# A hybrid encoder layer on one core: small TensorE products regrouped, weight splits in quarters, sums in PSUM, a ring of eight tiles

## The chip, the core and the metric

The kernel runs on one core of a Trainium2 chip. A core has TensorE (PE, the matrix products; PEld is its loading of weights), VectorE (DVE), ScalarE (ACT), GpSimd (POOL) and SyncE (SP), which here issues the weight transfers. The metric is the device time of one execution in microseconds (us). The kernel before takes 1457.91 us, the median of 3 runs (1456.87 to 1460.44).

## What is computed

One layer of an encoder trunk for 256 tokens of width 2048, all in float32. The reference, cut to what matters:

```
mod = silu(c) @ w_ada + b_ada                 # six vectors of 2048: shift, scale, gate, twice
h = rms_norm(x, g_mix) * (1 + sc1) + sh1
z = h @ w_in                                  # 2048 x 4616
y = concat[gmlp(u, v), pool(p), forgetting_attention(q, k, va, fz)] @ w_out
x = x + g1 * y
h = rms_norm(x, g_ffn) * (1 + sc2) + sh2
# router: scores = sigmoid(h @ w_router); the best of 4 groups, then its best 2 experts of 4
hid = silu(xb @ w_gate[e]) * (xb @ w_up[e])   # for the tokens of each of 16 experts
x = x + g2 * (scatter of hid @ w_down[e], times the gate)
```

The last 8 columns of `w_in` give `fz`, the forget logits, whose running sum over the tokens enters the attention scores as a bias.

## The kernel before, in words

Numbers are those of the profile's lines. The tokens lie in two halves of 128 (`h`), the width of 2048 in 16 slices of 128 (`k`).

*Weights.* They arrive in tiles of 1 MB, half of a ring tile each (`ring`, L140; six halves until the output projection, then eight), loaded by SP (`load_tile`, L144). There are two kinds. The matrix weights (`w_in`, `w_out`) are split by `split` (L173) into a rounded part on ScalarE (L174) and the rest on VectorE or GpSimd (L175), both in `whl`, and a product is three matmuls (`mm3`, L177). A tile of 512 rows by 512 columns is split in two halves of 128x1024 (`halves`, L407, and `small_piece`, L458); `WSPLIT` and `WSO` say which engine takes the second half's rest. The modulation weights (`w_ada`) go unsplit, either as matmuls with one row of output into an accumulator bank `accs[0]` or `accs[1]`, four slices on the four strips of 32 columns at once (`ada_parts`, L250), or as sums on VectorE in SBUF (`sum_parts`, L272: one operation for each slice, `ga` and `grow`). Which it is stands in `M1A` to `G1`.

*Order.* `step` (L155) issues a load and a split, and puts the work that uses them into a queue `todo`; when more than `LOOK` splits or `LOOK_ALL` loads are queued, the oldest is run. `PLAN` and `LAST` say behind which piece of `w_in` each modulation tile, each chunk's `make_h` and each step of the mixers stands.

*Stages.* The first stage runs over five chunks of slices (`CHUNKS`: 2, 2, 4, 4, 4 slices), since the shift and scale of a chunk are enough to make its part of `h`: the modulation rows of a chunk are copied out (`rows`, L304), turned into columns by four matmuls with one moving column (`cols`, L309), and `make_h` (L386) transposes `x` times the norm by `diag`, applies shift and scale, splits the result and multiplies it by the forget weights into `fzp`, one matmul of 8 rows for each slice (`late`). Then the nine pieces of `w_in` for that chunk are multiplied, each 24 matmuls into two `pm` banks, and added to `z` by `put` (L432). During the last chunk the modulation of the second half (`mod2`) and the mixers run in between: gMLP, pooling with the matrices of `band` (L366), attention in four steps (`att_a` to `att_d`), with the squares of each head summed by `squares` (L539).

The second stage is the output projection: four blocks `n` of 512 columns, four tiles each; behind a block `x1_block` (L836) multiplies by the gate (`xg`) and adds to `x`, then `logit_a` and `logit_b` transpose the new `x` and multiply it by the router weights, with the transposed `x` as the stationary operand. Beside blocks 0 to 2 VectorE sums the gate rows of the following blocks (`grow`), beside block 3 TensorE makes `g2`.

Then come the routing (L945 onwards: scores, group and expert choice, places of the tokens), the gathering of the tokens, and 15 expert places with 24 MB of weights each, whose loads can start only when the routing has written which expert stands where.

## Time and profile before

| | |
|---|---|
| median of 3 runs | 1457.91 us |
| the profiled execution | 1460.89 us |
| its span in the trace | 1459.1 us |
| TensorE busy, granted clock | 1264.6 us, 0.958 |
| VectorE, ScalarE, GpSimd busy | 693.5, 412.8, 146.0 us |
| DMA | 539.14 MB, mean 369 GB/s |

A row of a table by stage gives the length of a stretch, the busy time of PE, PEld, DVE, ACT and POOL with the number of instructions, the granted TensorE clock as a share of 2.4 GHz, the mean busy share of the DMA engines, and GB/s. A row of a timeline gives start, length, engine, line, operation, output and input, and in brackets how long the engine stood idle before it and what released it. A float32 matmul counts as two instructions there, a transpose or a product of split parts as one. Ends of matmuls are modelled and overlap the next start, so that a cost is read from start to start.

### The profile page before, as it was taken

The page shows a single profiled execution, that of the slowest core. Times are in us where ns is not written, and L with a number is a line of the kernel's source. Part 1 is how long each engine was busy: PE and PEld are TensorE (multiplying, and loading weights), DVE is VectorE, ACT ScalarE, POOL GpSimd, SP SyncE. Part 2 cuts the span into 40 slices and gives each one's busy share as a digit, 9 for nine tenths or more (in the row PEclk, how much of TensorE's full clock was granted, in tenths as well). Part 3 has the DMA queues.
Part 4 walks back from the last instruction along what each step waited for, and adds up shares of the span by engine and source line. Part 5 has one row for each costly group of instructions (what it writes and reads, how often), then busy time and mean ns, then how long its engine had stood idle before and what let it go on. Part 6 is the DMA issues. An engine that isn't in the chain of part 4 may idle for free.

```text
span 1459.1 us, 17581 instructions
## 1 busy us (share of the span) xinstructions
PE 1264.6 (87%) x6930; PEld 703.1 (48%) x6930; DVE 693.5 (48%) x1184; ACT 412.8 (28%) x720; POOL 146.0 (10%) x89
## 2 busy tenths in 40 slices
PE   5999999999989997999968999789997879858865
PEld 3666666666667563575324753337633222222221
DVE  3757483555798372795125961169711202202112
ACT  4433333646333240583003840028400000000000
POOL 0423332311333100000000000000000000000000
PEclk8999999999999998999999999999999999979988
DMA  9787787888877868998999989999899999999997
GB/s 378 270 348 281 281 340 265 303 351 328 349 278 270 310 288 367 427 428 317 421 426 427 426 318 419 424 428 426 333 408 428 427 426 427 428 426 428 426 426 303
DMA packets 49207, 539.14 MB, mean 369 GB/s; under 512 B 5464, under 2 KB 5592, under 8 KB 7008
## 3 DMA queue, kind: packets, MB, share of 16 engines
q1 hardware_dynamic: 47664, 534.79, 89.7%
q10 hardware_dynamic: 1456, 3.17, 0.6%
q8 instruction: 56, 0.92, 0.2%
q14 instruction: 31, 0.25, 0.0%
HBM read 535.85 MB, written 2.10 MB: 369 GB/s over the span
## 4 chain that ended last, share of the span: by engine, by line
PE 38%; DMA 27%; DVE 5%; issue 1%; ACT 1%; DVEq 0%; ACTq 0%
PE lbank L170 28%; DMA ring<-in_e_down_dram 11%; DMA ringl<-in_e_gu_dram 9%; DMA ring<-in_e_gu_dram 7%; PE bank L170 5%; PE pm L170 3%; DVE grow L292 2%; PE ada L170 1%; DVE whl L175 1%; DVE el L175 1%; ACT el L174 0%; DVE grow L290 0%; PE lgp L170 0%; DVE hid L1225 0%; PE pt L170 0%
## 5 line engine op out<-in xcount | busy, mean ns | idle before, releaser
L170 PE MATMUL pm<-whl,hT 128*128 128x512 f32 x1120 | 300.9, 405 | 19.9 <-DVE whl L175 10.8
L170 PEld LDWEIGHTS pm<-whl,hT 128*128 128x128 f32 x1120 | 212.3, 193 | 93.6 <-issue 15.3
L170 PE MATMUL lbank<-ringl,xr 128*32 128x256 f32 (+1 forms) x1152 | 143.7, 496 | 38.0 <-DMA ringl<-in_e_gu_dram 37.8
L170 PE MATMUL lbank<-el,xs 128*128 128x512 f32 x576 | 139.9, 401 | 10.2 <-ACT el L174 7.4
L170 PE MATMUL lbank<-ring,xr 128*32 128x256 f32 (+1 forms) x864 | 105.6, 491 | 34.1 <-DMA ring<-in_e_gu_dram 34.0
L174 ACT CAST whl<-ring 128x1024 fp32r<-128x1024 f32 x96 | 99.0, 1048 | 125.7 <-PE pm L170 70.7
L175 POOL TENSOR_TENSOR whl<-ring,whl 128x1024 fp32r<-128x1024 f32 x43 | 108.3, 2518 | 231.7 <-ACT whl L174 211.0
L170 PEld LDWEIGHTS lbank<-el,xs 128*128 128x128 f32 x576 | 109.3, 192 | 41.0 <-ACT el L174 10.6
L170 PE MATMUL bank<-y,gt 128*128 128x512 f32 x240 | 119.1, 619 | 0.0
L1284 DVE TENSOR_TENSOR xa<-xa,bank 128x512 f32<-128x512 f32 x120 | 82.5, 687 | 69.9 <-PE bank L170 69.9
L170 PEld LDWEIGHTS lbank<-ringl,xr 128*32 128x32 f32 (+1 forms) x1152 | 51.9, 128 | 129.8 <-issue 68.5
L170 PE MATMUL lbank<-ring,hidT 128*64 128x512 f32 (+1 forms) x576 | 103.8, 624 | 11.5 <-DMA ring<-in_e_down_dram 11.5
L1275 DVE TENSOR_TENSOR y<-lbank,g2w 128x512 f32<-128x512 f32 x60 | 41.5, 691 | 145.7 <-PE lbank L170 145.7
L174 ACT CAST el<-ring 128x512 fp32r<-128x512 f32 x144 | 89.7, 623 | 29.6 <-PE lbank L170 21.7
L175 DVE TENSOR_TENSOR el<-ring,el 128x512 fp32r<-128x512 f32 x144 | 92.7, 688 | 0.0
L175 DVE TENSOR_TENSOR whl<-ring,whl 128x1024 fp32r<-128x1024 f32 x53 | 72.2, 1368 | 35.9 <-ACT whl L174 33.6
L170 PE MATMUL ada<-ring,cact 128*1 128x512 f32 (+1 forms) x648 | 75.1, 566 | 15.6 <-DMA ring<-in_w_ada_dram 14.4
L1171 ACT COPY gt<-bank 128x256 f32<-128x256 f32 x15 | 5.6, 372 | 287.9 <-PE bank L1169 287.9
L170 PEld LDWEIGHTS lbank<-ring,xr 128*32 128x32 f32 (+1 forms) x864 | 39.5, 128 | 98.4 <-DMA ring<-in_e_gu_dram 48.4
L1225 DVE TENSOR_TENSOR hid<-hid,lbank 128x512 f32<-128x512 f32 x12 | 8.2, 687 | 165.0 <-PE lbank L170 164.7
L170 PE MATMUL lbank<-el,hidT 128*128 128x512 f32 x288 | 74.8, 411 | 12.2 <-DVE el L175 8.3
L438 DVE TENSOR_TENSOR z<-z,pm 128x512 f32<-128x512 f32 x72 | 49.0, 685 | 71.8 <-PE pm L170 71.8
(363 smaller groups left out, 1219.3 us busy)
## 6 DMA issues: line engine op xcount, KB each, us to landing
ringl<-in_e_gu_dram SPq DMA_DIRECT2D x60, 2048.0 KB, 20.1
ring<-in_w_ada_dram SPq DMA_DIRECT2D x90, 1024.0 KB, 7.0
ring<-in_e_gu_dram SPq DMA_DIRECT2D x45, 2048.0 KB, 24.4
ring<-in_e_down_dram SPq DMA_DIRECT2D x45, 2048.0 KB, 25.6
ring<-in_w_in_dram SPq DMA_DIRECT2D x35, 1024.0 KB, 7.0
ringm<-in_e_gu_dram SPq DMA_DIRECT2D x15, 2048.0 KB, 21.7
ringm<-in_e_down_dram SPq DMA_DIRECT2D x15, 2048.0 KB, 21.5
ring<-in_w_out_dram SPq DMA_DIRECT2D x12, 1024.0 KB, 8.3
```

What stands on the lines that cost most here:

```text
L170: E.matmul(out, lhsT=lhsT, rhs=rhs, start=start, stop=stop, skip_group_check=True)
L174: S.copy(hi, src)
L175: (eng or V).tensor_tensor(lo, src, hi.bitcast(F32), op=OP.subtract)
L292: eng.scalar_tensor_tensor(a, w[:, j, :], ck, a, op0=OP.mult, op1=OP.add)
L438: V.tensor_tensor(dst, dst, P[h], op=OP.add)
L1171: S.copy(gt, p[:, :256])
L1225: V.tensor_tensor(hid[:, o], hid[:, o], P[2 * b + 1], op=OP.mult)
L1275: V.tensor_tensor(y, P, g2w[:, c0:c0 + 512], op=OP.mult)
L1284: V.tensor_tensor(a, a, p, op=OP.add)
```

## The change

- `cols4` is new: the columns of a modulation row come by four transposes and a VectorE reduce over the four strips, where they came by four matmuls with a selecting column. `cols` stays for the rows that VectorE sums.
- `make_h` collects the forget matmuls of a chunk, and they run together two entries later in the queue.
- `logit_b` makes the router weights the stationary operand: four matmuls of 16 rows by 256 columns on four strips; at the end the four strips are copied out and added by two matmuls with `sel16`.
- Splits are in quarters (128x512); the look-ahead counts a quarter as 1 and a modulation tile as 2, up to 4; VectorE and GpSimd take the rests in turn.
- `sum_parts` sums into the accumulator banks in PSUM; the last operation writes SBUF.
- Two tiles `spare` join the ring until the last chunk; their room is then `ylo`'s.
- `band` becomes a loop on VectorE ahead of the first chunk; `squares` is one ScalarE operation into a `pt` bank and one reduce on VectorE for each half; `mod2`'s column steps stand two entries later.

```diff
-LOOK, LOOK_ALL = 2, 2
+LOOK, LOOK_SPLITS = 4, 6
-WSPLIT, WSO = "VGGGG", "G"
+WSPLIT, WSO = ["VGVG"] * 5, "VGVG"
...
-        while sum(p for _, _, p in todo) > LOOK or sum(x is not None for _, x, _ in todo) > LOOK_ALL:
+        while sum(0 if x is None else 1 if p else 2 for _, x, p in todo) > LOOK:
             run_first()
...
-    def sum_parts(sec, k0, nk, after, eng, tile_of, bias=None):
+    def sum_parts(sec, k0, nk, after, acc, eng, tile_of, bias=None):
+        P = accs[acc][:, :128 * nk]
...
                     if k == 0:
-                        eng.tensor_scalar(a, w[:, j, :], ck, None, op0=OP.mult)
+                        eng.tensor_scalar(P, w[:, j, :], ck, None, op0=OP.mult)
+                    elif k < KD - 1:
+                        eng.scalar_tensor_tensor(P, w[:, j, :], ck, P, op0=OP.mult, op1=OP.add)
                     else:
-                        eng.scalar_tensor_tensor(a, w[:, j, :], ck, a, op0=OP.mult, op1=OP.add)
+                        a = tile_of()[:, :128 * nk]
+                        eng.scalar_tensor_tensor(a, w[:, j, :], ck, P, op0=OP.mult, op1=OP.add)
...
+    def cols4(r4, nk):
+        p = pt()
+        for m in range(nk):
+            E.transpose(p[:, 128 * m:128 * m + 128], r4[:, 128 * m:128 * m + 128], ident)
+        c = wk.tile([128, 4], F32, name="c4")
+        V.tensor_reduce(c[:, :nk], p.rearrange("p (m j r) -> p m j r", j=4, r=32)[:, :nk, :, 0], AX.X, OP.add)
+        return c
...
+    sp, s_sp = pool("sp", 1, side="right")
+    spare = [sp.tile([128, RINGW], F32, name=f"spare{i}") for i in range(2)]
+    ring_tiles.extend(spare)
...
             split(hq[:, 0, c, :], hq[:, 1, c, :], t)
-            if late is not None:
-                late()
-
-            def late(k=k, t=t):
+            ts.append((k, t))
+
+        def late():
+            for k, t in ts:
                 o = 32 * (k % 4)
                 mm(fzp[o:o + 8, :], wfz[:, k, :], t, start=k < 4, stop=k >= KD - 4)
-        todo.insert(1, (late, None, False)) if todo else late()
+        todo.insert(2, (late, None, False)) if todo else late()
...
-                hl = hp.tile([128, 2, 2, 512], F32R, name="whl")
-                split(hl[:, 0], hl[:, 1], buf[0][:, 2 * a:2 * a + 2, :], engs[a])
+                hl = hp.tile([128, 2, 512], F32R, name="whl")
+                split(hl[:, 0], hl[:, 1], buf[0][:, a, :], engs[a])
...
-            for e in range(4):
-                S.activation(sqj, z[:, h, c0 + 128 * e:c0 + 128 * e + 128], AF.Square,
-                             accum_out=sst[key][:, i, h, e:e + 1])
+            p = pt()
+            S.activation(p, z[:, h, c0:c0 + 512], AF.Square)
+            V.tensor_reduce(sst[key][:, i, h, :], p.rearrange("p (e d) -> p e d", e=4), AX.X, OP.add)
...
-        mod2[i] = (mod2[i][0], 2 + (i // 4 - 1) % 2)
+        mod2[i + 2] = (mod2[i + 2][0], 2 + (i // 4 - 1) % 2)
...
-    mm(lgp.rearrange("p h e -> p (h e)"), maskb[:, :128], ident[:, :32], stop=False)
...
     def logit_b(n):
-        for a in range(2):
-            for c in range(2):
-                for h in range(2):
-                    k = 4 * n + 2 * a + c
-                    mm(lgp[:, h, :], x1T[n][a][:, 256 * c + 128 * h:256 * c + 128 * h + 128], wra[:, k, :],
-                       start=False, stop=k == KD - 1)
+        for j in range(4):
+            k = 4 * n + j
+            mm(lgp[32 * j:32 * j + 16, :], wra[:, k, :], x1T[n][j // 2][:, 256 * (j % 2):256 * (j % 2) + 256],
+               start=n == 0, stop=n == 3)
...
+    lgs = wk2.tile([128, 512], F32, name="x1T", bufs=2)[:, :256]
+    V.tensor_copy(lgs, lgp)
+    lg = pt()
     for h in range(2):
-        V.scalar_tensor_tensor(sc[:, h, :], lgp[:, h, :], rs1[:, h:h + 1], lconst, op0=OP.mult, op1=OP.add)
+        mm(lg[:, 16 * h:16 * h + 16], lgs[:, 128 * h:128 * h + 128], sel16)
+    for h in range(2):
+        V.scalar_tensor_tensor(sc[:, h, :], lg[:, 16 * h:16 * h + 16], rs1[:, h:h + 1], lconst, op0=OP.mult, op1=OP.add)
```

What stands in a row on TensorE where chunk 2 of `h` is made, before (`sel,r`: the columns of the scale; `diag,xa`: a transposed slice; `lgp<-hf`: a forget matmul; a count at the end: so many alike):

```order
L170 MATMUL pt_115<-sel,r_714 128x1 x4
L170 MATMUL pt_114<-diag,xa 128x128 x2
L170 MATMUL pt_115<-diag,xa 128x128 x2
L170 MATMUL lgp<-hf,prm_69 8x256
L170 MATMUL pt_114<-diag,xa 128x128 x2
L170 MATMUL lgp<-hf,prm_69 8x256
L170 MATMUL pt_115<-diag,xa 128x128 x2
L170 MATMUL lgp<-hf,prm_69 8x256
L170 MATMUL pm<-whl,hT_125 128x512 x12
L170 MATMUL lgp<-hf,prm_69 8x256
```

The same place in the changed kernel, on TensorE (`ident,r`: the transposes that replace the columns' matmuls):

```order
L324 MATMUL pt_120<-ident,r_769 128x128 x4
L171 MATMUL pt_119<-diag,xa 128x128 x2
L171 MATMUL pt_120<-diag,xa 128x128 x2
L171 MATMUL pt_119<-diag,xa 128x128 x2
L171 MATMUL pt_120<-diag,xa 128x128 x2
L171 MATMUL pm<-whl,hT_130 128x512 x12
L171 MATMUL lgp<-hf,prm_69 8x256 x4
```

The four forget matmuls have moved together behind two quarters of the first piece.

VectorE in chunk 2 before, where the third and fourth piece meet the shift's last tiles (`whl`: the rest of a split; `z<-z,pm`: the addition of a piece; `ga`: a sum):

```order
L175 TENSOR_TENSOR whl<-ring_64,whl 128x1024
L292 SCALAR_TENSOR_TENSOR ga<-ring_63,cact,ga 128x512 x4
L438 TENSOR_TENSOR z<-z,pm 128x512 x2
L175 TENSOR_TENSOR whl<-ring_63,whl 128x1024
L292 SCALAR_TENSOR_TENSOR ga<-ring_65,cact,ga 128x512 x4
L175 TENSOR_TENSOR whl<-ring_64,whl 128x1024
```

The same place on VectorE in the changed kernel:

```order
L294 SCALAR_TENSOR_TENSOR ada_113<-spare_138,cact,ada_113 128x512 x4
L176 TENSOR_TENSOR whl<-ring_63,whl 128x512
L451 TENSOR_TENSOR z<-z,pm 128x512 x2
L176 TENSOR_TENSOR whl<-ring_65,whl 128x512
L294 SCALAR_TENSOR_TENSOR ada_113<-ring_64,cact,ada_113 128x512 x3
L297 SCALAR_TENSOR_TENSOR ga<-ring_64,cact,ada_113 128x512
```

And on TensorE there, in the changed kernel (`ada_113`: the scale's first matmuls, into the bank that VectorE sums in; `ada_114`: a tile of the second half):

```order
L171 MATMUL ada_114<-ring_63,cact 1x512 x4
L171 MATMUL pm<-whl,hT_130 128x512 x24
L171 MATMUL ada_113<-ring_64,cact 1x512 x4
L171 MATMUL pm<-whl,hT_130 128x512 x24
L171 MATMUL ada_113<-ring_65,cact 1x512 x4
```

The sums have moved from `ga` into `ada_113`, one split now stands on each side of a piece's addition, and TensorE's next matmuls into `ada_113` stand behind the fourth piece, whose addition is the `z` row above.

The end of the projection on TensorE before (`ident,xa`: the transposes of the last block):

```order
L857 MATMUL pt_114<-ident,xa 128x128 x4
L170 MATMUL ada_109<-ring_65,cact 1x512 x4
L170 MATMUL lgp<-wra,x1T 128x16 x8
L170 MATMUL ada_109<-ring_65,cact 1x512 x4
L170 MATMUL ada_109<-ring_63,cact 1x512 x4
```

And in the changed kernel (`sel_91,x1T`: the two matmuls that add the strips):

```order
L873 MATMUL pt_119<-ident,xa 128x128 x4
L171 MATMUL ada_114<-ring_63,cact 1x512 x4
L171 MATMUL lgp<-x1T,wra 16x256 x4
L171 MATMUL pt_120<-sel_91,x1T 128x16 x2
L171 MATMUL ada_114<-ring_63,cact 1x512 x4
```

Two matmuls now stand between the last logits and the modulation tiles behind them.

## Rows read from the trace of the kernel before

**Rows 1.** Table by stage: length, PE, PEld, DVE, ACT, POOL, clock, DMA, GB/s

```profile
20.00:250.00 230.00, 217.72 (x1088) 149.83 (x1084) 139.97 (x188) 78.92 (x100) 72.65 (x44) 0.97 0.78 303
250.00:372.00 122.00, 118.47 (x715) 76.93 (x710) 65.56 (x158) 68.81 (x188) 27.29 (x21) 0.99 0.86 327
372.00:497.00 125.00, 113.88 (x541) 86.51 (x540) 90.41 (x82) 40.86 (x55) 45.34 (x20) 0.95 0.78 302
516.00:1459.00 943.00, 791.27 (x4403) 381.71 (x4402) 379.52 (x674) 211.00 (x357) 0.00 (x0) 0.95 0.96 403
```

**Rows 2.** TensorE's waits, 372 to 497 us: total, times, longest

```profile
PE pm L170 <- DVE xg L839: 7.0, 3, 3.1
PE pm L170 <- DVE whl L175: 3.8, 3, 2.3
```

**Rows 3.** TensorE's waits, 20 to 250 us

```profile
PE pm L170 <- DVE whl L175: 7.0, 6, 2.1
```

**Rows 4.** Timeline of VectorE in the output projection

```profile
417.29 3.10 DVE L292 SCALAR_TENSOR_TENSOR grow<-ring,cact,grow 128x512 f32<-128x512 f32 x4
...
422.04 5.22 DVE L292 SCALAR_TENSOR_TENSOR grow<-ring,cact,grow 128x512 f32<-128x512 f32 x4
```

**Rows 5.** Forms on two tiles: ns shortest/median/longest, first and last start

```profile
L292 DVE SCALAR_TENSOR_TENSOR ga<-ring,cact,ga x30: 739/752/2937, 113.9 to 204.0; 128x512 f32<-128x512 f32 x30
...
L438 DVE TENSOR_TENSOR z<-z,pm x56: 673/686/689, 66.6 to 246.9; 128x512 f32<-128x512 f32 x56
```

**Rows 6.** Timeline of TensorE, and table by stretch as in rows 1

```profile
434.87 0.72 PE L170 MATMUL pm<-whl,hT 128*128 128x512 f32 x1 [2.70 <-DVE xg L839]
...
465.17 0.50 PE L170 MATMUL pm<-whl,hT 128*128 128x512 f32 x1 [3.08 <-DVE xg L839]
...
375.00:380.00 5.00, 5.00 (x12) 3.94 (x13) 3.69 (x5) 0.38 (x1) 0.00 (x0) 0.50 1.01 419
435.00:438.00 3.00, 3.00 (x8) 2.33 (x9) 1.69 (x2) 1.79 (x5) 1.18 (x1) 0.50 0.90 339
465.00:469.00 4.00, 3.83 (x10) 3.08 (x11) 2.12 (x4) 2.49 (x6) 1.28 (x1) 0.59 0.90 358
```

**Rows 7.** Timeline of TensorE: four columns, and four transposes of attention

```profile
87.76 0.95 PE L170 MATMUL pt<-sel,r 128*128 128x1 f32 x8
88.64 1.04 PE L170 MATMUL ada<-ring,cact 128*1 128x512 f32 x8
...
285.30 0.60 PE L567 MATMUL pt<-ident,z 128*128 128x128 f32 x4
285.74 0.39 PE L170 MATMUL pt<-qk 128*128 128x128 f32 x2
```

**Rows 8.** Timeline of TensorE: eight modulation matmuls, a piece, a forget matmul

```profile
41.83 1.04 PE L170 MATMUL ada<-ring,cact 128*1 128x256 f32 x16
42.80 5.74 PE L170 MATMUL pm<-whl,hT 128*128 128x512 f32 x24
...
104.33 0.60 PE L170 MATMUL lgp<-hf,prm 128*8 128x256 f32 x2
104.86 0.71 PE L170 MATMUL pt<-diag,xa 128*128 128x128 f32 x4
```

**Rows 9.** Timeline: a block's logits on TensorE, the first scores on VectorE

```profile
423.40 1.85 PE L170 MATMUL lgp<-wra,x1T 128*128 128x16 f32 x16
425.10 0.48 PE L170 MATMUL pm<-whl,hT 128*128 128x512 f32 x1
...
502.01 0.38 DVE L949 SCALAR_TENSOR_TENSOR sc<-lgp,rs,lconst 128x16 f32<-128x16 f32 x2
```

**Rows 10.** Groups of the page: the experts' splits of 128x512, busy, mean ns

```profile
L174 ACT CAST el<-ring 128x512 fp32r<-128x512 f32 x144 | 89.7, 623 | 29.6 <-PE lbank L170 21.7
L175 DVE TENSOR_TENSOR el<-ring,el 128x512 fp32r<-128x512 f32 x144 | 92.7, 688 | 0.0
```

**Rows 11.** Timeline of TensorE in chunk 2

```profile
126.72 5.26 PE L170 MATMUL pm<-whl,hT 128*128 128x512 f32 x22 [1.51 <-DVE whl L175]
```

More of the change, by code (lines that the diff above doesn't have):

```diff
@@ L209, in body @@
         V.memset(sel[32 * j:32 * j + 1, :], 1.0)
+    sel16 = c1.tile([128, 16], F32, name="sel16")
+    V.tensor_copy(sel16, ident[:, 0:16])
+    for j in range(1, 4):
+        V.tensor_tensor(sel16, sel16, ident[:, 32 * j:32 * j + 16], op=OP.add)
     sel8 = c1.tile([128, 8], F32, name="sel8")
@@ L227, in body @@
     fzp = lgp[:, 256:512]
-    lgp = lgp[:, 0:32].rearrange("p (h e) -> p h e", h=2)
+    lgp = lgp[:, 0:256]
     def pm():
@@ L388, in make_h @@
         hq = hbuf(q)
-        late = None
+        ts = []
         for c in range(nk):
@@ L422, in run @@
                 for h in range(2):
-                    for c in range(2):
-                        xh, xl = xs(2 * a + c, h)
-                        mm3(P[h], xh, xl, hl[:, 0, c, :], hl[:, 1, c, :], first and a + c == 0, last and a + c == 2)
-                if a == 1:
+                    mm3(P[h], *xs(a, h), hl[:, 0], hl[:, 1], first and a == 0, last and a == 3)
+                if a == 3:
                     after(P)
             step(prep, run, True)
-        one(0)
-        one(1)
+        for a in range(4):
+            one(a)
     def put(q, c0, P):
@@ L453, in banks, with one @@
             return P
-        halves(win_d, WIN[q, c0], (V, WS[q]), lambda c, h: hpart(q, c, h), banks, True, True,
+        halves(win_d, WIN[q, c0], WS[q], lambda c, h: hpart(q, c, h), banks, True, True,
                lambda P: put(q, c0, P))
     def small_piece(q, c0, n):
-        buf = []
-        def one(a):
+        buf, P = [], []
+        def one(a, c):
             def prep():
-                if a == 0:
+                if a + c == 0:
                     w = ring()[:, :2 * n]
@@ L466, in prep @@
                     buf.append(w.rearrange("p (k n) -> p k n", k=2))
-                hl = hp.tile([128, 2, 2, 512], F32R, name="whl")
-                split(hl[:, 0], hl[:, 1], buf[0][:, :, 512 * a:512 * a + 512], (V, WS[q])[a])
+                hl = hp.tile([128, 2, 512], F32R, name="whl")
+                split(hl[:, 0], hl[:, 1], buf[0][:, c, 512 * a:512 * a + 512], WS[q][2 * (a % 2) + c])
                 return hl
             def run(hl):
-                P = [pm(), pm()]
+                if c == 0:
+                    P.extend([pm(), pm()])
                 for h in range(2):
-                    for c in range(2):
-                        mm3(P[h], *hpart(q, c, h), hl[:, 0, c, :], hl[:, 1, c, :], c == 0, c == 1)
-                put(q, c0 + 512 * a, P)
+                    mm3(P[2 * a + h], *hpart(q, c, h), hl[:, 0], hl[:, 1], c == 0, c == 1)
+                if c:
+                    put(q, c0 + 512 * a, P[2 * a:])
             step(prep, run, True)
         for a in range(n // 512):
-            one(a)
+            for c in range(2):
+                one(a, c)
     hold = {}
@@ L707, in body @@
                 piece(q, PIECES[i])
-            if q == 0 and i < 4:
-                then(lambda i=i: band(i))
             for c in PLAN[q][i]:
@@ L723, in body @@
     tbanks.append(accs[0])
+    for t in spare:
+        while ring_tiles[-1] is not t:
+            ring_tiles.rotate(-1)
+        ring_tiles.pop()
+    s_sp.close()
+    py, s_py = pool("py", 1, side="right")
+    ylo = py.tile([128, KD, T], F32R, name="ylo")
     work = {
```

61 lines of the change are left out of this document (26 added, 35 removed).

## The prediction

> **What bounds the kernel now.** I read the busy time by stage first [rows 1]. From 516 us to the end the experts run, and there the DMA engines are busy 0.96 of the time at 403 GB/s: weights arrive as fast as they can. The change doesn't touch that stage, and its first load can't start before the routing is known. So whatever is won or lost before 516 us moves the end by the same amount. Before 516 us it is the other way round: from 20 to 497 us the DMA share is 0.78 to 0.86, and TensorE is busy 217.7 of 230, 118.5 of 122 and 113.9 of 125 us. The reader is to see stages where DMA has 14 to 22% to spare, VectorE 28 to 46% and ScalarE 44% or more, and where TensorE works nearly without a hole. Two things can be had there: shorter TensorE work, and the holes.
>
> The holes come next, in the list of waits. In the output projection (372 to 497 us) TensorE stands 7.0 us for `xg`, the DVE multiplication that frees the accumulator banks, and 3.8 us for `whl`, the split weights [rows 2]. From 20 to 250 us it stands 7.0 us for `whl` [rows 3]. All of these are VectorE being late. The timeline of VectorE tells why: four sums of `grow` take 3.10 us at 417.29, but 5.22 us at 422.04 [rows 4]. The form list says the same: a sum takes 752 ns in the median and up to 2937 ns, while `z<-z,pm`, which has one operand in PSUM, stays between 673 and 689 ns in all 56 cases [rows 5], though GpSimd is busy a third of that stretch [rows 1]. So operations with both inputs in SBUF are held up beside GpSimd, and those with one PSUM operand are not.
>
> After the longest of these waits the clock is low as well: after the wait of 2.70 us at 434.87 the granted clock is 0.50 (1.2 GHz) for 3 us, 0.50 for 5 us from 375, 0.59 for 4 us from 465 [rows 6]. Half of such time is lost: 2.5 + 1.5 + 1.6 = 5.6 us.
>
> **The change part by part**, against the profiled execution (1460.9 us; its span is 1459.1).
>
> *Columns by transposes.* Four columns of a modulation row are now four matmuls with one moving column each; from their start to the next instruction 87.76 to 88.64 = 0.88 us [rows 7]. The four 128x128 transposes of attention are the same form as the new ones and take 285.30 to 285.74 = 0.44 us [rows 7]. The order shows twelve sets of four and four sets of two that change (the two sets behind a VectorE sum keep the old form): 12 x 0.44 + 4 x 0.22 = 6.2 us of TensorE. VectorE gets 16 small reduces more; they stand ahead of the `mod` additions, about 0.2 us each, where TensorE has the `diag` products to do.
>
> *Forget logits by chunk.* Sixteen matmuls of 8 rows stand singly between others: 104.33 to 104.86, 0.53 us each, 8.5 us in all [rows 8]. In the new order they follow one another in each chunk, on four different strips of columns. What that gives is shown by the modulation matmuls, one row each, 256 columns, on the same four strips: eight of them take 41.83 to 42.80 = 0.97 us, so a round of four costs 0.5 us [rows 8]. Five chunks, five rounds: 2.5 us, a saving of 6.0.
> The Trainium skill ("TensorE: Matmul & The Clock Gate", "Measured speedup vs the span model") gives 2.38 times for three column tiles, short of three. By an estimate from that, four strips would run 3.2 times as fast as one after another, a round would cost 0.66 us, and the nine rounds here and in the next part would save 1.4 us less; the trace's modulation matmuls do better than the page, 8 x 0.53 / 0.97 = 4.4 times.
>
> *Router weights stationary.* Eight matmuls with 16 moving columns and a 128x128 weight load each take 423.40 to 425.10 = 1.70 us per block of 512 columns [rows 9]. They become four of 256 columns on four strips, by the same row 0.5 us: 3 x 1.2 = 3.6 us saved in the first three blocks, and the 0.2 us matmul that cleared the bank. The fourth stands at the end, where the scores start at 502.01 [rows 9] behind the root of the norm, so its saving there is worth nothing; and behind it come a copy of 256 columns from PSUM (half the width of `z`'s 0.69 [rows 5], so 0.4 to 0.5), two small matmuls at 0.53 at most each [rows 8] and two hand-overs. I take 1.3 us longer for the routing chain. TensorE's remaining modulation work now waits behind those two matmuls, which costs the same time once, not twice. Net 2.5 us.
>
> *Sums in PSUM.* The trace has no VectorE sum into PSUM. Bounds: 0.69 us (`z<-z,pm` [rows 5]) and 1.3 (a quarter of the stretched 5.22 [rows 4]). I take the unstretched 0.75, nearer to `z`, since it too has one SBUF input. Of the projection's waits and lost clock, 7.0 + 3.8 + 5.6 = 16.4 us, most should go: a block of 512 columns has 16 sums (12.0 us), 8 split quarters (5.5) and five more operations of that width (3.5 by the row of `z`): 21 us of VectorE against 96 matmuls, 22.7 us at 5.7 for 24 (the 5.74 at 42.80 [rows 8]), and some 2 us of small ones on TensorE. I leave 1.7 us of the first wait (2.3 today; VectorE does routing constants ahead of it, and the split is now half as long) and 0.2 us at each bank change: 16.4 - 2.3 = 14.1 won. Bounds 8 (the clock not won back) to 16.4.
>
> *The new wait.* The sums now share accumulator `ada_113` with TensorE. In chunk 2 (CHUNKS[2], 110 to 170 us) the order has the last sum right behind a piece and TensorE's next use of that bank right behind the same piece. VectorE must first add that piece to `z` (0.69 [rows 5]), split a quarter (0.69 [rows 10]) and do four sums (3.0): with hand-overs TensorE stands 4.6 us, and every matmul queued behind it with it. At that length it restarts at the low clock, 1.5 us more [rows 6]. In chunk 3 a whole piece (24 matmuls, 5.7 us) lies between and hides the sums. Of the 7.0 us of `whl` waits [rows 3], chunk 2 has two, 1.51 at 126.72 [rows 11] and one like it of 1.93; shorter splits and unstretched sums leave about 1.4 there (VectorE needs 0.7 + 1.4 + 0.7 + 3.0 = 5.8 us for a piece of 5.7, so it stays just late) and 0.8 elsewhere. Sum: 1.4 + 0.8 + 4.6 + 1.5 - 7.0 = 1.3 us lost.
>
> *Splits in quarters.* For half the width there are rows from the experts: ScalarE 623 ns, VectorE 688 ns [rows 10]. A tile then costs ScalarE 2.5 us and VectorE 1.4 us, GpSimd about 2.5, beside 24 matmuls of 5.7 us; nobody becomes the bound. The cover is those 5.7 us; without it the longest of the three, 2.5 us, would show on each tile. The look-ahead keeps its bytes (four quarters for two halves). Nil.
>
> *Ring of 8, bands ahead of time, squares by two operations.* The heads of the two lists of waits stand in [rows 2, 3], and no DMA is in them: TensorE doesn't wait for a tile there, so two more tiles give nothing. The bands (24 short VectorE operations, some 6 us by my estimate) fall where VectorE waits for the first modulation; at worst 1 us is late. The squares take ScalarE work away and give VectorE ten reduces, between 250 and 372 us, where it is busy 65.6 of 122 us [rows 1]. Nil, one microsecond either way.
>
> Sum: 6.2 + 6.0 + 2.5 + 14.1 - 1.3 = 27.5 us. That is 1433.4 us against the profiled execution, which lies 3 us above the median of the runs; against the median 1457.9 it is 1430.
>
> **The rivals.**
> *TensorE's freed time comes back, the holes stay* (VectorE is still late at the banks, through the reduces and the finer splits in its queue): 6.2 + 6.0 + 2.5 - 1.3 = 13.4 us, 1444.5. For it: VectorE is busy 90 of 125 us there and its queue is in order. Against it: `z` is never stretched.
> *The strips don't overlap* for 8- and 16-row weights (the change doesn't do what it says): 6.0 lost, and logits 16 x 0.53 = 8.5 instead of 2.0, of which the last block counts little: 11 us less, 1441.5. Against it: the modulation rows.
> *Slower: sums into PSUM are slow.* One mechanism: each sum reads and writes PSUM, and VectorE becomes the bound in chunks 2 and 3 and in the projection. A block then costs 9.0 + 16x us with x per sum, against 434.87 to 465.17 = 30.3 today [rows 6]; a piece 2.8 + 4x (two splits and two additions of 0.69) against 5.7 and its share of the waits, 0.9; the hand-over 1.6 + 4x. Three blocks, eight pieces and the hand-over give 3 x (9 + 16x - 30.3) + 8 x (2.8 + 4x - 6.6) + 1.6 + 4x = 84x - 92.7 us, and what is won outside them is about 10: it turns at x = 1.22. At twice my price (1.5) the kernel is 23 us slower: 1481. Against it: `z` at 0.69 with a PSUM operand.
> *More than forecast*: no low clock at the new wait, no wait at the projection's start, 1420.
>
> **How the numbers follow.** Forecast 1430 (1423 to 1438 with its own bounds): 0.60. Holes stay, 1444: 0.16. No overlap, 1441: 0.07. Better, 1420: 0.07. Slower, 1481: 0.05. The gains are used up by waits I haven't seen, 1458: 0.05. The range reaches from the good case, 1420, to the holes' case with its own spread, 1448. About 0.3% (4.4 us) is what a measurement of this kernel can tell from no change: faster 0.88, same 0.06, slower 0.06.
>
> **What would show it.** Right: the routing's end at about 489 instead of 516 us with an unchanged stretch behind it; `z`-like durations (0.7 to 0.8 us, hardly a stretched one) for the sums; `xg` waits below 1 us in all; transposes of 0.44 us per four; one TensorE wait of 4 to 5 us on the sum's last step in chunk 2. Wrong: sums over 1.2 us; `lgp` groups of four at 2 us; waits on `pt` banks from the squares; a stretch behind the routing that is not 943 us.

## The result, and the profile after

The changed kernel takes 1439.01 us, the median of 4 runs (1435.49 to 1442.07); the kernel before took 1457.39 us in the 4 runs beside it. The ratio is 0.9874, with a 95% interval of 0.9848 to 0.9899. Faster was forecast, at 1430, with a range of 1420 to 1448: the direction and the range hold, but 18 us came (20.1 in the profiles, up to the first expert load) where 27.5 were forecast.

Three marks cut the trace where the forecast's terms meet: TensorE's first product with `ylo` opens the output projection, the start of its last `pm<-whl` product closes it, and SP's first load of expert weights starts the stretch that the DMA engines bound. Behind that load both kernels take as long, 942.6 us before and 943.8 after [rows 1], so all is decided ahead of it.

| stretch | before | after | forecast | measured |
|---|---|---|---|---|
| to the first product with `ylo` | 372.26 | 358.29 | -10.9 | -14.0 |
| the projection | 123.66 | 112.46 | -17.9 | -11.2 |
| last product to first expert load | 20.54 | 25.64 | +1.3 | +5.1 |
| sum | 516.46 | 496.39 | -27.5 | -20.1 |

VectorE's forms in the changed kernel, as in rows 5: the sums, and the rests of the splits.

```profile
L294 DVE SCALAR_TENSOR_TENSOR ada<-ring,cact,ada x54: 742/756/757, 105.5 to 434.8; 128x512 f32<-128x512 f32 x54
...
L176 DVE TENSOR_TENSOR whl<-ring,whl x86: 677/693/1803, 25.4 to 450.2; 128x512 fp32r<-128x512 f32 x86
```

No sum is stretched any more: the longest takes 757 ns, where one in SBUF took up to 2937 [rows 5]. The splits, with two inputs in SBUF, are still held up, to 1803 ns. The Trainium skill ("SBUF — State Buffer", "Who interferes with whom") says that a VectorE instruction with two SBUF inputs contends with a GpSimd instruction that reads SBUF, and one with at most one does not; these two rows agree.

The new wait in chunk 2, on TensorE and on VectorE:

```profile
120.06 2.56 PE L171 MATMUL pm<-whl,hT 128*128 128x512 f32 x10 [0.65 <-DVE whl L176]
127.04 1.04 PE L171 MATMUL ada<-ring,cact 128*1 128x512 f32 x8 [4.41 <-DVE ga L297]
128.01 7.29 PE L171 MATMUL pm<-whl,hT 128*128 128x512 f32 x24
```

```profile
121.98 1.37 DVE L451 TENSOR_TENSOR z<-z,pm 128x512 f32<-128x512 f32 x2 [1.97 <-PE pm L171]
123.27 0.68 DVE L176 TENSOR_TENSOR whl<-ring,whl 128x512 fp32r<-128x512 f32 x1
123.87 2.33 DVE L294 SCALAR_TENSOR_TENSOR ada<-ring,cact,ada 128x512 f32<-128x512 f32 x3
126.24 0.75 DVE L297 SCALAR_TENSOR_TENSOR ga<-ring,cact,ada 128x512 f32<-128x512 f32 x1
```

It is the forecast's wait, 4.41 us for 4.6: VectorE idles 1.97 us for the piece's end, and then adds, splits and sums while TensorE stands. The 24 products behind it take 7.29 us instead of 5.7.

TensorE's waits in the projection (358 to 471 us), as in rows 2:

```profile
PE pm L171 <- DVE xg L855: 3.7, 3, 1.8
PE pm L171 <- DVE whl L176: 3.0, 1, 3.0
```

7.0 + 3.8 us have become 3.7 + 3.0. Behind the projection 5.1 us were lost where 1.3 were forecast; TensorE there:

```profile
474.98 1.04 PE L171 MATMUL lgp<-x1T,wra 128*16 128x256 f32 x8
477.69 0.62 PE L171 MATMUL pt<-sel,x1T 128*128 128x16 f32 x4 [1.68 <-DVE x1T L963]
478.24 2.38 PE L171 MATMUL ada<-ring,cact 128*1 128x512 f32 x16
480.56 1.86 PE L171 MATMUL ada<-bgt,ident 8*1 8x512 f32 x2
482.35 3.59 PE L171 MATMUL ada<-ring,cact 128*1 128x512 f32 x16
...
488.79 0.62 PE L171 MATMUL pt<-M,ones 128*128 128x16 f32 x4
...
495.26 1.01 PE L171 MATMUL ada<-bgt,ident 8*1 8x512 f32 x2
```

VectorE has `M` ready at 484.79, yet TensorE's products on it start at 488.79, since its `g2` tiles run until then, some at half the clock (1.90 us for 16 entries at the high one). And who releases the first expert load? SP's queue, its start and its waits:

```profile
496.39 0.89 SPq L1312 DMA_DIRECT2D ringl<-in_e_gu_dram  x2
```

```profile
SPq L1316 <- DVE pos L1045: 11.2, 1, 11.2
...
SPq L1312 <- PE ada L171: 3.6, 1, 3.6
```

Its last wait is 3.6 us for TensorE's last modulation product (495.26 + 1.01), not for the routing's `pos`, which is ready at 492.18. It was so before the change too: `pos` at 512.24, the last product's end at 516.34, the load at 516.46. TensorE's queue is the path at the end of the routing.

### The profile page after: what moved, and what is told of

It reads as the page before. It is cut to its first block, busy times and chain, and to the rows that moved or that the text cites. A ratio compares the mean times of both kernels' runs of the same rounds, so it can differ in the third digit from the quotient of the medians.

```text
span 1440.2 us, 17629 instructions
## 1 busy us (share of the span) xinstructions
PE 1247.2 (87%) x6844; PEld 683.4 (47%) x6844; DVE 693.2 (48%) x1271; ACT 417.1 (29%) x754; POOL 160.5 (11%) x127
## 4 chain that ended last, share of the span: by engine, by line
PE 59%; DMA 26%; DVE 7%; issue 3%; ACT 2%; POOL 1%; SPq 0%; DVEq 0%; ACTq 0%; POOLq 0%
PE lbank L171 29%; PE pm L171 18%; DMA ring<-in_e_down_dram 11%; DMA ringl<-in_e_gu_dram 7%; DMA ring<-in_e_gu_dram 7%; PE bank L171 6%; PE ada L171 4%; PE pt L171 1%; DVE ada L294 1%; DMA ring<-in_w_ada_dram 1%; DVE whl L176 1%; DVE el L176 1%; ACT whl L175 1%; DVE z L451 1%; POOL whl L176 0%
## 5 line engine op out<-in xcount | busy, mean ns | idle before, releaser
L171 PE MATMUL pm<-whl,hT 128*128 128x512 f32 x1120 | 296.6, 400 | 9.7 <-DVE whl L176 3.9
L171 PEld LDWEIGHTS pm<-whl,hT 128*128 128x128 f32 x1120 | 208.8, 190 | 82.9 <-issue 12.8
L176 POOL TENSOR_TENSOR whl<-ring,whl 128x512 fp32r<-128x512 f32 x86 | 120.0, 1407 | 225.4 <-ACT whl L175 201.9
L175 ACT CAST whl<-ring 128x512 fp32r<-128x512 f32 x172 | 99.9, 622 | 72.6 <-PE pm L171 62.5
L171 PE MATMUL lbank<-ring,hidT 128*64 128x512 f32 (+1 forms) x576 | 104.6, 630 | 10.9 <-DMA ring<-in_e_down_dram 10.9
L176 DVE TENSOR_TENSOR whl<-ring,whl 128x512 fp32r<-128x512 f32 x86 | 83.9, 991 | 38.0 <-ACT whl L175 37.7
L171 PE MATMUL ada<-ring,cact 128*1 128x512 f32 (+1 forms) x568 | 68.6, 585 | 19.7 <-DMA ring<-in_w_ada_dram 14.0
L175 ACT CAST el<-ringl 128x512 fp32r<-128x512 f32 x96 | 58.7, 624 | 79.5 <-DMA ringl<-in_e_gu_dram 64.8
## 6 DMA issues: line engine op xcount, KB each, us to landing
ringl<-in_e_gu_dram SPq DMA_DIRECT2D x60, 2048.0 KB, 20.1
```

The lines of the kernel that those rows point to most:

```text
L171: E.matmul(out, lhsT=lhsT, rhs=rhs, start=start, stop=stop, skip_group_check=True)
L175: S.copy(hi, src)
L176: (eng or V).tensor_tensor(lo, src, hi.bitcast(F32), op=OP.subtract)
```

## The experiments

Each but one starts from the changed kernel. Single runs of one kernel spread by 2 to 11 us, so stretches of the trace decide on terms of a few microseconds. From the first expert load to the end all profiles show 939.5 to 945.0 us. The expectations name the start of the gathering's second half as the routing's end; it is 500.09, 502.27, 500.46 and 510.14 us in the first four kernels. It proved a poor measure: it contains a low clock that comes and goes (last section), so that the stretch from the last product to the first expert load varies from 22.4 to 27.3 us where nothing was changed in it. The readings below go by the stretches ahead of it.

### One part undone: columns, forget logits, logits, sums

**cols_back**

```diff
-            hold[i] = lambda: fin(cols4(r4, nk))
+            hold[i] = lambda: fin(cols(r4, nk, sel))
```

> The changed kernel with one part undone: the columns of the modulation rows come from four matmuls with one moving column again instead of four transposes and a reduce. Measure: the routing's end, which is the start of the second half's gathering product (499.12 us in the changed kernel, 519.18 before). Theory: a set of four is 0.88 instead of 0.44 us on TensorE and nothing else changes, 12 x 0.44 + 4 x 0.22 = 6.2 us: routing's end 505.3, time about 1445. Rival A: TensorE waits for the reduces (0.95 us for c in the list of waits, and hand-overs), so that the part is worth 3 to 4 us only: 502.5. Rival B: the 3 us by which the stretch before the projection came out better than forecast belong to this part: 508.5.

1441.45 us (ratio 0.9873). The projection opens at 359.91 (+1.6), though the first piece starts 1.0 us earlier: the part is worth 2.6 us, below rival A. Why can be seen where chunk 2 is made, on TensorE with transposes (the changed kernel) and with matmuls (this one), and on VectorE in the changed kernel:

```profile
92.46 0.60 PE L324 MATMUL pt<-ident,r 128*128 128x128 f32 x4
92.90 0.61 PE L171 MATMUL pt<-diag,xa 128*128 128x128 f32 x4
94.10 0.71 PE L171 MATMUL pt<-diag,xa 128*128 128x128 f32 x4 [0.59 <-DVE c L326]
```

```profile
91.53 0.95 PE L171 MATMUL pt<-sel,r 128*128 128x1 f32 x8
92.33 0.69 PE L171 MATMUL pt<-diag,xa 128*128 128x128 f32 x4
```

```profile
92.68 1.27 DVE L451 TENSOR_TENSOR z<-z,pm 128x512 f32<-128x512 f32 x2
93.88 0.16 DVE L326 TENSOR_REDUCE c<-pt 128x4 f32<-128x16 f32 x1
94.08 0.16 DVE L338 TENSOR_TENSOR mod<-c,prm 128x4 f32<-128x4 f32 x1
94.54 0.55 DVE L411 TENSOR_SCALAR hf<-pt,mod 128x256 f32<-128x256 f32 x1
```

Four transposes do take 0.44 us, but at a chunk's turn VectorE's additions and then its chain to `hf` are what is waited for, with the reduce now in it. What TensorE saves there it waits. Of the 2.6 us 1.9 come in the last chunk (132.35 for 134.21 us), where eight of the twelve sets of four stand and the forecast had 3.5: TensorE saves 3.2 on them and waits 0.8 longer in all.

**forget_back**: `make_h` runs each forget matmul behind the next slice again.

```diff
-            ts.append((k, t))
+            if late is not None:
+                late()
...
-            for k, t in ts:
+            def late(k=k, t=t):
```

> The changed kernel with one part undone: each forget matmul stands singly again, behind the next slice of its chunk, instead of all of a chunk together. Theory: 16 x 0.53 us against five rounds of 0.5 to 0.55, 5.7 to 6.0 us: routing's end 505.0 (499.12 in the changed kernel). Rival A: the strips hardly overlap, or the single matmuls fill time in which TensorE waits for the next slice's split: 1 to 2 us, 500.5. Rival B: the single ones also hold up make_h, and the 3 us by which the stretch before the projection came out better than forecast belong here: 508.

1443.22 us (0.989). The projection opens at 364.44, 6.15 us later, of which 1.6 are a low clock (0.69 from 242 to 247 us, 1.00 at that place in the changed kernel). Chunks 0 and 1 are as long as with the part (67.4 us), the others 1.2, 1.4 and, without the clock, 2.0 longer: 4.6 us in all. A round on four strips takes 0.55 us (99.91 to 100.46 in the changed kernel), so the price was right; but of the two-slice chunks nothing comes. By the estimate worked out from the Trainium skill's factor ("TensorE: Matmul & The Clock Gate", "Measured speedup vs the span model") a round would have been 0.66; the measured one is shorter.

**logit_back**

```diff
-            mm(lgp[32 * j:32 * j + 16, :], wra[:, k, :], x1T[n][j // 2][:, 256 * (j % 2):256 * (j % 2) + 256],
+                    mm(lgq[:, h, :], x1T[n][a][:, 256 * c + 128 * h:256 * c + 128 * h + 128], wra[:, k, :],
...
-    V.tensor_copy(lgs, lgp)
```

> The changed kernel with one part undone: in the router logits the transposed x is the stationary operand again, eight matmuls of 16 columns for each half block, with no strips to add at the end. Theory from the trace: the first three blocks lose 3 x 1.15 us (1.70 against 0.55) and 0.2 for the cleared bank, but the end wins back 5.1 us (from the last block's first modulation tile to the routing's end 22.94 us before, 28.05 now): routing's end 497.6, TensorE's wait for the copy of the logits gone, and the matmuls on M within 0.5 us of M's being ready. Rival, the step of the forecast (3.6 + 0.2 won, 1.3 lost): 501.6, with the end still as long as now, since it is long for another reason.

1440.32 us (0.986), no difference that the times could tell. In the trace both halves of the theory are there: the projection is 1.7 us longer (114.19), not 3.65, because `xg` waits shrink from 1.74 to 1.09 us at two bank changes; the stretch behind it is 2.9 us shorter (22.79), and TensorE reaches `M` 0.4 us after it is ready. But 1.6 of the 2.9 us are low clock, of which both profiles have some in this stretch, in different places. Where the clock is high as far as `M`, TensorE goes from the projection's last product to its first product on `M` in 13.50 us here (475.29 to 488.79) and in 14.75 with the part, in scale_later (466.78 to 481.53): 1.25 us, the forecast's 1.3. The part's net worth is 0.5 us by that, and below zero in the changed kernel's profile, where 2.5 were forecast.

**gate_sums_sbuf**

```diff
+        sb = bias is not None
...
+                P = buf[0] if sb else P0
```

> The changed kernel with the 48 sums of the gate rows in SBUF again; the sums of the first stage stay in PSUM. Theory: sums are stretched again beside GpSimd (some to 2.9 us), VectorE comes late to the banks, and the output projection gets back what it won besides the logits: from its first matmul to the modulation tile behind its last block it is 109.4 us now and was 121.3 before, of which 3.4 are the logits, so +8.5: routing's end 507.6. By the size in the forecast (14.1): 513. Rival: the quarters of the splits, taken in turn by VectorE and GpSimd, did it, and the place of the sums matters little: 499 to 501, with sums that are hardly stretched.

1452.59 us (0.995). The projection is 122.85 us, 10.4 longer. The sums' form, and TensorE's waits there:

```profile
L298 DVE SCALAR_TENSOR_TENSOR grow<-ring,cact,grow x33: 739/752/1798, 364.8 to 440.4; 128x512 f32<-128x512 f32 x33
```

```profile
PE pm L171 <- DVE xg L859: 8.2, 3, 3.8
PE pm L171 <- DVE whl L176: 3.0, 1, 3.0
```

With the same quarters and the same queue, the place of the gate rows' sums alone raises the `xg` waits from 3.7 to 8.2 us; most of the other 5.9 us are low clock behind two of them (0.66 from 389 to 394, 0.58 from 448 to 456; 1.00 behind all three in the changed kernel). The rival falls.

### One part alone

**sums_psum_alone** is the kernel before with `sum_parts` of the changed one (the edit is that function's part of the diff).

> The kernel before with one part of the change alone: the modulation sums of VectorE are in the accumulator banks in PSUM; halves of splits, ring, logits, columns and forget products stay as before. Measure: from the first product with ylo to the start of the last product of the projection, 123.7 us before, 112.5 in the changed kernel. Theory: the place of the sums does it nearly all: 113 to 115, sums unstretched at 0.75 us; and in chunk 2 a wait of about 4 us on the sum's last step appears, so that chunk 2 is longer than its 67.2 us of before. Rival: halves of 128x1024, stretched on VectorE, still hold up the banks and the quarters are needed too: 118 or more.

1451.96 us (0.9948). The projection takes 116.07 us, 7.6 less than before and just outside the theory's band. In it lies a stretch of half clock behind no wait, in none of the others' projections:

```profile
479.00:485.80 6.80, 6.80 (x19) 5.50 (x19) 0.00 (x0) 0.37 (x1) 0.00 (x0) 0.50 0.51 212
```

It costs 3.4 us, more than the 1.9 that lie between this projection and that of the changed kernel with the old logits (114.19). So these two profiles don't show that the quarters are worth anything there. Sums are 743 to 757 ns, and the wait appears here too:

```profile
134.59 1.89 PE L170 MATMUL ada<-ring,cact 128*1 128x512 f32 x8 [4.95 <-DVE ga L292]
```

Chunk 2 grows from 67.2 to 73.3 us, so 6.1 us of the sums' gain go there: most of it for this hand-over, some for a low clock (0.70 from 122 to 127 us) behind a `whl` wait ahead of it. `xg` waits are 0.69 us here, one multiplication, against 1.74 with the finer splits: a bank change with its multiplication cost no less than that in these two profiles.

### Parts priced at nothing

**ring_six**

```diff
-    ring_tiles.extend(spare)
```

> The changed kernel without the two extra ring tiles: six ring tiles until the output projection, as before. Measure: the first product with ylo, which opens the output projection (358.3 us in the changed kernel, 372.3 before), and chunks 0 and 1, from the first piece to the first transposed slice of chunk 2 (25.45 to 92.90 = 67.5 us; before 27.06 to 101.65 = 74.6). Theory of the forecast: two more tiles are worth nothing, since TensorE waits for no tile there: 67.5 and 358.3, each within 1 us. Rival: in chunk 0 the DMA engines are busy all the time now (1.01, 0.84 before), so the extra tiles take in weights that chunks 1 and 2 then don't wait for: 70 to 72, and 361 to 363.

1439.49 us (0.9866). Chunks 0 and 1 take 67.43 us: nil, as forecast. The projection opens 2.6 us later, but that arises in chunk 2, at the hand-over (5.07 us, then 0.50 of the clock for 5 us, 0.66 in the changed kernel), and it is as late in logit_back, which has the full ring. In chunk 0 the DMA share falls to 0.83 to 0.89 between 36 and 52 us, from 1.02 with the two extra tiles; nobody waits for what these bring.

**bands_back**: `band` of the kernel before, behind the first four pieces.

```diff
+            if q == 0 and i < 4:
+                then(lambda i=i: band(i))
```

> The changed kernel with the pooling matrices made during chunk 0 again, by VectorE and GpSimd, instead of ahead of it by VectorE. Measure: chunks 0 and 1, 67.5 us in the changed kernel and 74.6 before. Theory: in the kernel before, the last band's four operations (2.7 us) stood on VectorE's queue ahead of the first columns' addition, TensorE waited 0.96 us for it and 1.11 us for a split, and went on at a lower clock: 70 us, with such a wait at the first transposed slice of chunk 1. Rival, the forecast's nil: 67.5, and the 7 us of difference in these two chunks have to do with the quarters and the clock at the start.

1449.35 us (0.9941), 10 us lost. Chunks 0 and 1 take 79.96 us, more than in the kernel before; neither expectation saw it. TensorE, and GpSimd ahead of the first of the waits:

```profile
38.73 1.20 PE L171 MATMUL pm<-whl,hT 128*128 128x512 f32 x4 [2.58 <-POOL whl L176]
48.26 2.07 PE L171 MATMUL pm<-whl,hT 128*128 128x512 f32 x4 [2.59 <-POOL whl L176]
58.56 1.20 PE L171 MATMUL pm<-whl,hT 128*128 128x512 f32 x4 [1.77 <-POOL whl L176]
```

```profile
30.63 0.34 POOL L386 IOTA hf<- 128x256 f32 x1
34.78 0.73 POOL L390 TENSOR_TENSOR band<-hf,tri 128x256 f32<-128x256 f32 x1 [3.80 <-DVE hf L389]
...
37.41 1.26 POOL L176 TENSOR_TENSOR whl<-spare,whl 128x512 fp32r<-128x512 f32 x1
```

GpSimd waits 3.80 us for VectorE's part of a band, with a split queued behind it. In the kernel before, `WSPLIT` gave all rests of chunk 0 to VectorE, so nothing of TensorE's stood behind a band; with "VGVG" two quarters of each tile do. Moving the bands is what the quarters need; what it gives with the old splits was not run.

### What the terms that went wrong are worth

**scale_later**

```diff
-    ["n", "n", "nm", "nn", "n", "n", "n", "0m", "1h"],
+    ["n", "n", "nm", "n", "nn", "n", "n", "0m", "1h"],
```

> The changed kernel, with the scale's first modulation tile of chunk 2 one piece later in the plan, so that 24 matmuls lie between the shift's last sum and TensorE's next use of that accumulator bank. Measure: chunk 2, from the first transposed slice of its h to that of the next chunk: 92.90 to 162.96 = 70.1 us in the changed kernel. Theory of the hand-over: the wait of 4.41 us on the last sum goes, and the low clock behind it (1.5 us in that trace, up to 4 in the ones since) with it: 64 us, and the end moves by 6. Rival: VectorE is the bound over the four pieces with sums (four sums, two splits and two additions are 5.8 us for a piece of 5.7), and TensorE waits for whl where it waited for the sum: 68 us, the end 2 earlier.

1430.24 us (0.9804, interval 0.9783 to 0.9825), 8.8 us below the changed kernel. Chunk 2 takes 64.46 us, 5.6 less; TensorE there now:

```profile
117.07 3.02 PE L171 MATMUL pm<-whl,hT 128*128 128x512 f32 x12 [1.04 <-DVE whl L176]
120.71 8.01 PE L171 MATMUL pm<-whl,hT 128*128 128x512 f32 x34 [0.61 <-DVE whl L176]
```

The rival's waits are there, 1.65 us in all, but not in place of the 4.41. The first expert load comes 7.3 us earlier: 5.6 from here, 3.3 from the end (22.35 us instead of 25.64, where the clock stayed high), less 1.5 us in the last chunk, where it was 0.67 over 5 us behind a wait of 1.35 us. Only the 5.6 are the edit's.

**tail_mend**

```diff
+    def mid(copy):
+        copy()
+        logit_b(3)
+        V.tensor_copy(lgs, lgp)
+
-    logit_a(3, root_x1)
+    logit_a(3, lambda copy: root_x1(lambda: mid(copy)))
     g2_run(G2_MID)
-    logit_b(3)
```

> The changed kernel, with the last block's logits, and the copy of the four strips behind them, placed on VectorE's queue ahead of the four small operations that finish the norm's root (which wait for ScalarE anyway), and the modulation tile that stood before the logits placed behind them. Measure: from the start of the last product of the projection (470.75) to the routing's end (499.12): 28.4 us in the changed kernel, 23.3 before. Theory: the wait of 1.68 us for the copy falls below 0.5, TensorE goes on at the high clock, its matmuls on M start within 0.7 us of M's being ready: 24.0 us. Rival: the low clock at this place comes from the many small matmuls and not from the wait, 27 us.

1440.06 us (0.9879). To the gathering's second half 26.98 us: the theory's 24.0 is missed. Its first part holds: no wait ahead of `sel`, and `M`'s products start 0.7 us after `M`. But then the clock falls, behind a wait of 1.03 us that was there before:

```profile
488.51 0.60 PE L171 MATMUL pt<-ohc,ec 16*128 16x16 f32 x2 [1.03 <-DVE ohc L1039]
489.04 6.52 PE L171 MATMUL ada<-ring,cact 128*1 128x512 f32 x32
495.49 1.01 PE L171 MATMUL ada<-bgt,ident 8*1 8x512 f32 x2
```

6.52 us for 32 entries that take 3.61 at the high clock: what was saved ahead of `M` is lost behind it. The rival's 27 us are met, but not as it had it: ahead of `M` the clock stays high. Why it falls behind `ohc` here, and not in the changed kernel, stays open.

**consts_later**: `wra`, `revc`, `triE`, `capR`, `limR` and GpSimd's index rows in a function called at

```diff
+            if n == 0 and g == 1:
+                consts()
```

> The changed kernel, with the constants of the routing (GpSimd's six index rows, VectorE's wra, revc, triE, capR and limR) issued behind the second tile of the output projection instead of ahead of its first split. Measure: from the first product with ylo (358.29) to block 1's first wait (389.15): 30.9 us in the changed kernel. Theory: VectorE reaches the first rests some 2.6 us earlier, the wait of 2.97 us falls to 0.5, and the half clock of the twelve matmuls behind it, 2.5 us, goes too: 26 us. Rival: the wait is one on the first tile's transfer or on ScalarE's cast, or the constants hold up the splits of the second and third tile as long: 29 to 31.

1439.81 us (0.9874). From the first product with `ylo` to block 1 28.25 us instead of 30.86: between theory and rival. VectorE in the changed kernel, ahead of the wait of 2.97 us:

```profile
358.44 1.41 DVE L826 TENSOR_TENSOR triE<-ioE,ioR 128x256 f32<-128x256 f32 x1
...
359.94 1.07 DVE L834 TENSOR_SCALAR limR<-capR 128x16 f32<-128x16 f32 x1
360.92 2.96 DVE L176 TENSOR_TENSOR whl<-ring,whl 128x512 fp32r<-128x512 f32 x3
```

Without the constants TensorE waits 1.15 us, and the clock behind it is 0.66 for 5 us instead of 0.50. In the times the gain doesn't show, and the projection opens 1.6 us later than in the changed kernel, with a low clock in the last chunk (0.69 over 5 us from 237.6).

**mended** has these three edits.

> The three edits scale_later, tail_mend and consts_later together. Theory: they lie in three different stretches, all before the routing's end, so they add: 6 + 4.4 + 4.9 = 15 us, routing's end at 484 to 486 us instead of 499.1, time 1423 to 1426, ratio to the kernel before 0.977. Rival: the time won early is given back as waits for weights, since transfers start earlier by less: routing's end 491 or later, DMA share above 0.95 from 360 us on.

1428.45 us (0.9805, interval 0.9784 to 0.9825; 5 runs, 1427.93 to 1433.12). The gathering comes at 486.52, 12.6 us earlier, just outside the theory's 484 to 486, and the time misses its 1423 to 1426. The low clock behind `ohc` is there (6.30 us for 3.61), as in tail_mend. The times don't tell it from scale_later alone.

**best** adds two edits for that end:

```diff
-                    mm(P[0:1, :], ident[0:8, bias:bias + 1], bgt, start=False)
+                    mm(P[0:1, :], ident[0:8, bias:bias + 1], bgs[-1], start=False)
...
-    oneh = wide_ring[-1][:, :1024].rearrange("p (h s) -> p h s", h=2)
+    oneh = wide_ring[-1][:, RINGW:RINGW + 1024].rearrange("p (h s) -> p h s", h=2)
```

> The kernel with the three mended places (scale later, logits ahead of the root's end, constants later), and two more edits for the end of the routing: the bias rows that TensorE adds to g2 are read from a copy in memory that the experts' first tile doesn't take over, and the placement matrix stands in the half of its ring tile that the last modulation tile doesn't use. Theory: the first load of expert weights and the placement matrix then no longer wait for TensorE's last modulation products; the load starts within 1 us of VectorE's pos instead of behind the last bias product, 3 us earlier than with the three edits (484.1), at 479 to 481 us, the gathering at about 484, and the time is 1423 to 1426. Rival: the load waits for another reader of that memory or the transfers of the last modulation tiles, and starts at 484 as with the three edits: 1428.

1426.42 us (6 runs, 1423.55 to 1427.31; ratio 0.977, interval 0.9742 to 0.9799), 0.4 us above the theory's band, with every run below all of mended's, and 31 us less than the kernel before. VectorE's `pos`, SP's first load, and TensorE's last bias product:

```profile
480.11 0.19 DVE L1056 COPY pos<-pt 128x48 f32<-128x48 f32 x1
```

```profile
480.92 0.89 SPq L1323 DMA_DIRECT2D ringl<-in_e_gu_dram  x2
```

```profile
486.02 1.01 PE L171 MATMUL ada<-bgs,ident 8*1 8x512 f32 x2
486.96 3.29 PE L171 MATMUL pm<-ring,xa 128*128 128x256 f32 x14
```

The load starts 0.8 us behind `pos` and 6 us ahead of TensorE's end; from the projection's last product it takes 18.09 us, where mended has 24.36 (the projection itself closes 3 us later than there). 943.8 us from it to the end are what the other kernels show. So it was that product, through the memory of `bgt`, that held the load. The second edit came with it and was not run apart; it bears on `ring`, where VectorE waited 2.25 us for TensorE in mended before it wrote the placement matrix and no longer does, while the load goes into `ringl`. The gathering is later than expected (486.96 for 484), since it stands behind the modulation on TensorE's own queue; that costs nothing.

## Why the prediction was right or wrong

*What bounds the kernel*: right. What was won before the first expert load came off the end (20.1 us there, 18.9 in the span), and the stretch behind it didn't change. But that the first load can't start before the routing is known names the earlier of two conditions: it starts behind TensorE's last `g2` product, 4.2 us after `pos`.

*Columns*, 6.2 forecast, 2.6 measured. The step took TensorE's time, from a set's start to the next instruction, for the path. At a chunk's turn VectorE is the path, and the cover that the forecast named for the reduces ("TensorE has the `diag` products to do") ends after one slice, with 0.59 us of wait. In the last chunk about half of it came.

*Forget logits*, 6.0 forecast, 4.6 measured without the clock: price and overlap right, the two-slice chunks give nothing.

*Router logits*, 2.5 forecast, about 0 measured. Two steps failed. In the blocks TensorE's saving was taken for the path: 1.7 came for 3.8, the rest ran into `xg` waits. At the end the 1.3 us were right at the high clock (1.25, by logit_back), but the sum had no term for the clock. The modulation tiles behind the two matmuls are themselves the path to the load, and of the 5.1 us lost in the changed kernel's profile 3.3 are their low clock (25.64 against 22.35 us in the profiles whose clock stays high there). Another 0.6 of the 5.1 are not the logits': TensorE waits 0.78 us for `xa` ahead of the last transposes, where it waited 0.28, and does so with the old logits too. Nor is it shown that the logits cause the low clock: in logit_back, tail_mend, mended and best the wait for the copy is gone, and the clock falls behind `ohc` instead.

*Sums in PSUM and the projection*: mechanism right, price right (0.756 for 0.75), 10.4 us by the undone part and 7.6 alone, with 3.4 us lost to a half clock behind no wait in it. The term of 14.1 was too large at two places. First wait: 1.7 forecast, 2.97 measured and 2.5 us of half clock behind it,

```profile
361.00:366.00 5.00, 4.34 (x10) 3.46 (x11) 4.43 (x7) 0.62 (x1) 1.74 (x1) 0.50 1.01 426
```

because the constants ahead of it (named in the forecast, but not counted out) are 1.8 us of it, and the three rests behind them are stretched. Bank changes: 0.2 each forecast, 1.75 at two of three, 3.1 us too much in all. With 1.3 for the first wait and 2.5 for the clock these are 6.9 us, what the projection fell short (6.7). VectorE is still 1.0 us late there and needs 0.7 for the multiplication itself:

```profile
413.34 0.75 DVE L297 SCALAR_TENSOR_TENSOR grow<-ringm,cact,ada 128x512 f32<-128x512 f32 x1
414.12 0.74 DVE L300 SCALAR_TENSOR_TENSOR grow<-bgt,ident,grow 8x512 f32<-8x512 f32 x1
414.79 1.27 DVE L855 TENSOR_TENSOR xg<-pm,g 128x512 f32<-128x512 f32 x2
```

*The new wait*: right in place, cause and size; without it chunk 2 is 5.6 us shorter, by the forecast 6.1 (4.6 + 1.5).

*Parts at nil*: the ring, yes. The bands, no: in the quartered kernel their old place costs 10 us; the forecast's cover for the quarters ("nobody becomes the bound") held only because the bands had gone. The squares and the later column steps of `mod2` were not undone. That the stretch to the projection came out 3.1 us better than forecast lies in chunks 0 and 1, 7.1 us shorter:

```profile
28.00:76.00 48.00, 45.20 (x240) 30.02 (x241) 30.50 (x38) 23.08 (x34) 16.66 (x21) 0.93 0.73 273
```

```profile
28.00:76.00 48.00, 46.87 (x268) 31.70 (x267) 19.23 (x30) 27.07 (x51) 17.82 (x14) 1.00 0.95 387
```

Before (the first row) the granted clock is 0.93 from 28 to 76 us, after it 1.00; the forecast had looked for lost clock in the projection alone. Of the 7.1 us, 2.2 are no part of the change: sums_psum_alone, with the program of before in these chunks, has 72.4 us instead of 74.6. How the other 5 divide among halves, bands and the chunk's turn was not taken apart. Another 1.6 us lie ahead of the first piece (27.06 before, 25.45 after), whose start moves between 24.27 and 25.76 among the changed kernels, so they can't be put down to the change. That the total came within the range is in part luck: gains that no term had, in these two chunks, stand against 6.7 us missing in the projection and 3.8 behind it.

*Rivals*: the measured time lies between the forecast and "the holes stay" (1444.5), and so do the projection's holes: 3.7 + 3.0 us of 7.0 + 3.8. That the strips don't overlap is refuted by 0.55 us for a round of four, and slow sums by 0.756 us, where it turned at 1.22.

## What to carry to other kernels

Price a small product by who waits at its place, not by its own time: what TensorE saved at a chunk's turn or in front of a late bank went into the next wait. When work is divided finer over two engines, look at what else stands on the newly added engine's queue. And look for what really releases the transfer that opens the bound stage: here it was a 1 us product that read memory about to be reused, and with a copy the load came 6 us sooner behind the projection.

## What was not expected of the hardware

The same wait doesn't always cost the clock. TensorE waits 1.67 to 1.68 us for the strips' copy in eight of these profiles; over the 8 us behind it the granted clock was 0.57, 0.58, 0.58 and 0.79 in four (gate_sums_sbuf, the changed kernel, consts_later, cols_back) and 1.00 in the other four (forget_back, scale_later, ring_six, bands_back). Waits of 4.4 to 5.1 us on the last sum were followed by 0.50 to 0.71 over 5 us every time, those of 1.74 on `xg` never by less than 1.00. In sums_psum_alone it fell behind no wait at all: 0.50 from 479.0 to 485.8 us, when TensorE had been busy for all of the 4 us before with one-row modulation products, two products with `ones` and the logits' 16-column products; before the change it stays at 1.00 there. So a profile's stretch behind a wait of 1 to 3 us can be off by 3 us, and one profile of each kernel doesn't settle a term of that size; stretches that agree in several do.
